# Ending each layer's down projection by token halves, with a norm for each half

## The chip, the cores and the metric

The kernel runs on one core of one Trainium2 chip. The metric is the time of one execution in microseconds of device time, lower is better. The engines are PE (matrix multiply, with its weight loads), DVE (elementwise, reductions), ACT (activations, casts, copies), POOL, and SP, which here only issues DMA transfers. Each engine works through its own instructions in the order in which they were placed, and an instruction that waits holds up those behind it on the same engine.

## The reference

Two layers of a hybrid encoder over 256 tokens of width 2048, float32. Cut to what matters:

```
h = x                                           # (1, 256, 2048)
h = h + pool_mixer(rms_norm(h, norm1_g[0]))     # layer 0
h = h + swiglu_ffn(rms_norm(h, norm2_g[0]))     # w1, w3: 2048 x 5632, w2: 5632 x 2048
h = h + rwkv7_time_mix(rms_norm(h, norm1_g[1])) # layer 1
h = h + swiglu_ffn(rms_norm(h, norm2_g[1]))
return rms_norm(h, final_g)

rms_norm(x, g)   = x * rsqrt(mean(x * x over the width) + 1e-6) * g
swiglu_ffn(h)    = (silu(h @ w1) * (h @ w3)) @ w2
```

The time mixing is six token-shifted mixes, projections by w_r, w_k, w_v, low-rank maps for decay, rate and gate, a recurrence over 256 tokens for 32 heads of size 64 (computed here in chunks, with triangular systems that are inverted step by step), a group norm, a gate and the projection w_o.

## The kernel before

The 256 tokens are two halves i = 0, 1 of 128 rows (partitions), the width four column groups n = 0..3 of 512. `h[i][n]` is a 128x512 tile that stays on the chip from start to end (the trace calls it `base`, like everything in that large buffer). Each float32 operand of a product is split into a high and a low part: a weight tile `raw` (128x1024, loaded on SP's queue at L151, four buffers) is cast to `wh` on ACT (L152) and `wl = raw - wh` is taken on DVE (L153), with two buffers of each (`kwh`, `kwl`, `vh`, `vl` are the same in other buffers). A product is then three matmuls: high by high, low by high, high by low.

`ffn(layer)` ends with the down projection, the loop `for two in range(2)`. One pass makes two column groups n0, n1 for both halves in four accumulators `C[i][m]`, over 22 steps p of 256 rows of w2. Eighteen steps run first (seven of them in a form with fewer products and extra accumulators, which are added to `h` on DVE). The last four, p = 18 to 21, run as `columns(p, m)`: all four for the first column group (m = 0), then all four for the second (m = 1), for both halves at once. Behind each column group stand the additions `h[i][n] += C[i][m]` on DVE (L426) and the sums of squares on ACT (L164, tile `junk`); in the second layer also the multiplication by the final gain (L1101). `rstd_of_h` makes the reciprocal root of both halves in one go: a reduction (L171), a square root on ACT (L172, whose table of functions has to be loaded), a reciprocal and a Newton step on DVE (L173 to L182). `load_sqrt`, right behind the up projections, is there to request that table early; its argument is a constant, so nothing ties it to that place.

After the first layer's FFN, `rwkv` starts with `hs[i] = h[i][n] * rstd`, two PE transposes per block of 128 columns into one PSUM tile, an evacuation with the gain on ACT (L666, 16 of them, 128x256), mixes on DVE and then the projections (PE from L736). Behind the projections, from about 1100 to 1400 us, the recurrence is worked off chunk by chunk beside the projection w_o: `KB` and `AR` are loaded per chunk (L832, L833), Gram products `g` and `G` are made, `sv`, `vt`, `rhs`, `cb` are the chunk's vectors, S the state, y the output, which is normed (L976 to L996; `ysq` is its square on ACT, L980) and transposed on PE (L1002). The triangular systems of one half of the chunks are inverted together on DVE: `sysM` is loaded from `dM`, then pairs of L633 (`sysP`) and L634 (`sysZ`) follow one another, and the result goes out to `dZ` and comes back as `Z`.

After the second layer's FFN, `rstd` scales `h` (DVE L1111 for the first half, ACT L1109 for the second) and eight stores of 256 KB go out, four on ACT's queue, four on SP's.

The order on each engine is not written out. A scheduler with its own time model puts the instructions of the whole program in order when the program is built, so an edit in one place can change the order elsewhere.

Of the kernel before, what the change touches and what calls it, by code (L numbers as in the profile page):

```python
# [37 lines left out]
GC, G7 = 1, 0  # L38
# [54 lines left out]
def hybrid_encoder(ctx: ExitStack, tc: tile.TileContext, I, out):  # L93
# [156 lines left out]
    def ffn(layer, each=None):  # L250
        gcol = par[f"g2_{layer}"]
        with ExitStack() as st:
# [4 lines left out]
            rb = base[:, 4864:]  # L257
# [79 lines left out]
            load_sqrt(epsr[:, 0:1])  # L337
# [112 lines left out]
    def rwkv():  # L450
        with ExitStack() as st:
# [192 lines left out]
            with tc.tile_pool(name="rp1", bufs=1) as p1:  # L644
                rstd = rstd_of_h()
                hn = []
                hn_ = p1.tile([128, 16, 257], F32, name="hn")
                for n in range(4):
                    hs = []
                    for i in range(2):  # L650
                        s_ = mx(F32, "hs")
                        if i and n < HSA:
                            nc.scalar.activation(s_, h[i][n], AF.Copy, scale=rstd[:, i:i + 1])
                        else:
                            nc.vector.tensor_scalar(s_, h[i][n], rstd[:, i:i + 1], None, ALU.mult)
                        hs.append(s_)
                        nc.sync.dma_start(dH[i][n], h[i][n])
                    for q in range(4):
                        k = n * 4 + q
                        tp = g_bank()  # L660
                        for i in range(2):
                            nc.tensor.transpose(tp[:, i * 128:(i + 1) * 128], hs[i][:, q * 128:(q + 1) * 128], ident)
                        t_ = hn_[:, k]
                        with queued("newton"):
# [501 lines left out]
```

## Time and profile before

| | us |
|---|---|
| three runs | 2180.53, 2188.81, 2189.13 (median 2188.81) |
| profiled execution | 2181.9 |
| its span in the trace | 2180.1 |
| mean granted TensorE clock | 0.981 of full |
| PE busy | 2116.9 (97% of the span) |
| DVE busy | 1553.9 (71%) |
| ACT busy | 1147.3 (53%) |
| last matmul of the first down projection | starts at 780.61 |
| stretch of the recurrence | about 1100 to 1400 |
| last matmul of the program | starts at 2166.50 |

A row of the trace's order in time gives the start in us, the duration, engine, line, operation, out<-in, the shape and how many such instructions were joined in the row; in brackets stands the idle time of the engine just before it and what ended that. A clock of 1.00 is TensorE's level of 2.4 GHz, 0.50 that of 1.2 GHz.

### The profile page before, as it was taken

To read this page: it belongs to the slowest core of one execution; us is meant where nothing else is said; L and a number is where in the kernel's file an instruction comes from. 1 tells how busy PE (TensorE), PEld (TensorE's weight loads), DVE (VectorE), ACT (ScalarE), POOL (GpSimd) and SP (SyncE) were. 2 spreads that over 40 slices of the span, in tenths; PEclk is the share of its full clock that TensorE was granted. 3 is DMA by queue.
4 is the path that set the end of the run, shared out by engine and by line. 5 is a ranking of instruction groups with operands and counts; after the bars stand their busy time and mean duration, and the time that the engine had idled before them with its cause. 6 is when DMAs were issued, how large, how long until landed. Compare 5 with 4: busy or idle time off the path is not lost.

```text
span 2180.1 us, 34748 instructions
## 1 busy us (share of the span) xinstructions
PE 2116.9 (97%) x13318; PEld 1843.5 (85%) x13318; DVE 1553.9 (71%) x2548; ACT 1147.3 (53%) x1884; POOL 30.6 (1%) x72
## 2 busy tenths in 40 slices
PE   7999999999999989999999999999999999999997
PEld 5888888888878879999988778788888888888786
DVE  8666666666787978688866767876666666677886
ACT  5544444444555478766745354554444444445444
POOL 0000000000000000011000000000000000000000
PEclk9999999999999999999998699999999999999999
DMA  6555565665566645466565343446666666655654
GB/s 232 174 187 191 186 191 187 190 187 190 196 198 217 207 155 163 163 210 207 171 218 151 108 121 105 160 121 191 188 189 189 188 189 189 188 191 199 204 202 156
DMA packets 147478, 395.11 MB, mean 181 GB/s; under 512 B 39280, under 2 KB 46832, under 8 KB 147056
## 3 DMA queue, kind: packets, MB, share of 16 engines
q1 hardware_dynamic: 146160, 390.80, 56.2%
q8 instruction: 104, 1.70, 0.3%
q10 hardware_dynamic: 1152, 2.10, 0.3%
q14 instruction: 62, 0.51, 0.1%
HBM read 376.59 MB, written 16.25 MB: 180 GB/s over the span
## 4 chain that ended last, share of the span: by engine, by line
PE 86%; DVE 6%; DMA 4%; ACT 2%; issue 1%; SPq 0%; ACTq 0%; DVEq 0%
PE acc L311 29%; PE acc L347 17%; PE acc L313 15%; PE acc L691 2%; PE acc L689 2%; PE acc L690 2%; DVE wl L153 2%; PE tp L347 2%; PE acc L1022 1%; PE acc L1024 1%; PE acc L1023 1%; DMA raw<-in_w 1%; PE acc L516 1%; PE acc L515 1%; PE cb L907 1%
## 5 line engine op out<-in xcount | busy, mean ns | idle before, releaser
L153 DVE TENSOR_TENSOR wl<-raw,wh 128x1024 fp32r<-128x1024 f32 (+1 forms) x525 | 640.2, 1220 | 432.2 <-ACT wh L152 428.0
L152 ACT CAST wh<-raw 128x1024 fp32r<-128x1024 f32 (+1 forms) x525 | 548.5, 1045 | 648.7 <-PE acc L311 276.9
L311 PE MATMUL acc<-xs,wh 128*128 128x512 f32 x2816 | 710.6, 393 | 3.7 <-DVE xs L266 3.2
L311 PEld LDWEIGHTS acc<-xs,wh 128*128 128x128 f32 x2816 | 504.9, 189 | 94.9 <-DVE xs L266 5.1
L313 PEld LDWEIGHTS acc<-xs,wl 128*128 128x128 f32 x2816 | 384.1, 190 | 27.5
L313 PE MATMUL acc<-xs,wl 128*128 128x256 f32 x2816 | 392.7, 282 | 0.0
L347 PE MATMUL acc<-vh,gT 128*128 128x512 f32 x640 | 184.9, 390 | 0.8 <-ACT vh L152 0.8
L347 PEld LDWEIGHTS acc<-vh,gT 128*128 128x128 f32 x640 | 119.7, 188 | 27.3 <-ACT vh L152 2.6
L691 PE MATMUL acc<-mx,wl 128*128 128x256 f32 x464 | 133.0, 287 | 3.5 <-DVE wl L153 3.5
L689 PE MATMUL acc<-mx,wh 128*128 128x256 f32 x464 | 132.1, 285 | 0.0
L690 PE MATMUL acc<-mx,wh 128*128 128x256 f32 x464 | 131.8, 284 | 0.0
L153 DVE TENSOR_TENSOR vl<-raw,vh 128x1024 fp32r<-128x1024 f32 x80 | 95.5, 1221 | 27.1 <-ACT vh L152 19.7
L347 PE MATMUL acc<-vl,gT 128*128 128x512 f32 x320 | 112.2, 389 | 0.0
L152 ACT CAST vh<-raw 128x1024 fp32r<-128x1024 f32 x80 | 80.9, 1050 | 49.3 <-PE acc L347 22.7
L355 ACT CAST vh<-T 128x1024 fp32r<-128x1024 f32 x56 | 58.9, 1052 | 80.5 <-DVE T L397 43.6
L347 PE MATMUL acc<-wh,gT 128*128 128x512 f32 x320 | 93.8, 390 | 0.7 <-ACT wh L152 0.7
L691 PEld LDWEIGHTS acc<-mx,wl 128*128 128x128 f32 x464 | 88.5, 191 | 5.3 <-DVE wl L153 5.2
L689 PEld LDWEIGHTS acc<-mx,wh 128*128 128x128 f32 x464 | 88.5, 191 | 0.8
L690 PEld LDWEIGHTS acc<-mx,wh 128*128 128x128 f32 x464 | 88.6, 191 | 0.0
L347 PE MATMUL acc<-vh,g 128*128 128x512 f32 x280 | 77.9, 391 | 1.1 <-ACT vh L355 0.6
L516 PE MATMUL acc<-wl,mx 128*128 128x256 f32 x256 | 74.2, 290 | 1.2 <-DVE wl L153 1.1
L515 PE MATMUL acc<-wh,mx 128*128 128x256 f32 x256 | 74.2, 290 | 0.0
(329 smaller groups left out, 3118.5 us busy)
## 6 DMA issues: line engine op xcount, KB each, us to landing
raw<-in_w SPq DMA_DIRECT2D x528, 512.0 KB, 4.4
raw<-in_wk SPq DMA_DIRECT2D x32, 512.0 KB, 3.7
raw<-in_wr SPq DMA_DIRECT2D x32, 512.0 KB, 3.7
raw<-in_wv SPq DMA_DIRECT2D x32, 512.0 KB, 4.0
raw<-in_wo SPq DMA_DIRECT2D x32, 512.0 KB, 3.6
raw<-in_pw SPq DMA_DIRECT2D x8, 512.0 KB, 7.8
dKB<-KB SPq DMA_DIRECT2D x16, 256.0 KB, 3.1
dKB<-AR SPq DMA_DIRECT2D x16, 256.0 KB, 3.7
```

The lines of the kernel that those rows point to most:

```text
L152: nc.scalar.copy(wh[:P, :step], raw[:P, :step])
L153: nc.vector.tensor_sub(wl[:P, :step], raw[:P, :step], wh[:P, :step].bitcast(F32))
L311: nc.tensor.matmul(acc, lhsT=w[:, cs], rhs=xs[q * 4 + kk], start=(q + kk == 0), stop=False, skip_group_check=True)
L313: nc.tensor.matmul(acc[:, :256], lhsT=l[:, cs], rhs=xs[q * 4 + kk][:, :256], start=False, stop=(q + kk == 6), skip_group_check=True)
L347: nc.tensor.matmul(out_, lhsT=lhsT, rhs=rhs, start=start, stop=stop, skip_group_check=True)
L355: nc.scalar.copy(wh, src)
L515: nc.tensor.matmul(av[:, i], lhsT=xh, rhs=w[:, cs], start=(k == 0 and i == 0), stop=False, skip_group_check=True)
L516: nc.tensor.matmul(av[:, i], lhsT=xh, rhs=l[:, cs], start=False, stop=False, skip_group_check=True)
L689: nc.tensor.matmul(acc[:, :256], lhsT=w[:, cs], rhs=xs[k][:, :256], start=(k == 0), stop=False)
L690: nc.tensor.matmul(acc[:, :256], lhsT=w[:, cs], rhs=xs[k][:, 256:], start=False, stop=False)
L691: nc.tensor.matmul(acc[:, :256], lhsT=l[:, cs], rhs=xs[k][:, :256], start=False, stop=(k == 15))
L907: nc.tensor.matmul(cb[:, jj, 0, hc], lhsT=g_[jj][u % 2][k_, c], rhs=rows_of(u)[k_], start=(u == 0), stop=False, skip_group_check=True)
```

## The change

In the last pass of each down projection the last LH steps (two in the first FFN, one in the second) change their order: the split weights of these steps are kept, and all their products for the first 128 tokens stand ahead of all those for the second. Each half then gets its own additions, squares and `rstd` (one column instead of two), in both layers. The scaling after the first FFN, the transposes and the evacuation go by halves too: four transposes of one half fill a PSUM tile, six of the eight tiles are evacuated on DVE by one multiplication with a broadcast gain (L685, 128x4x128), the other two on ACT by four activations each (L683). At the end the scalings and stores go by halves, with odd column groups on ACT and SP's queue. The gain is multiplied per half, too. `load_sqrt` now takes a value from the last `gT` tile, which ties the request of the root's table to the end of the up projections.

```diff
-GC, G7 = 1, 0
+GC, G7, LH = 1, 0, (2, 1)
-    def rstd_of_h():
-        at = 4624 + 4 * next(counter)
-        s, r = base[:, at:at + 2], base[:, at + 2:at + 4]
-        nc.vector.tensor_reduce(s, ssp, AX.X, ALU.add)
+    def rstd_of_h(i=None):
+        at, w = 4624 + 4 * next(counter), 2 if i is None else 1
+        s, r = base[:, at:at + w], base[:, at + 2:at + 2 + w]
+        nc.vector.tensor_reduce(s, ssp if i is None else ssp[:, i:i + 1], AX.X, ALU.add)
...
-            load_sqrt(epsr[:, 0:1])
+            load_sqrt(gT[FT - 1][0][0][:, 0:1].bitcast(F32))
...
+            def finish(i, n, acc):
+                nc.vector.tensor_add(h[i][n], h[i][n], acc)
+                square_sums(i, n)
+                if each is not None:
+                    each(i, n, lambda: ff.tile([128, 512], F32, name="g4" if n % 2 else "t4", tag="g4" if n % 2 else "t4", bufs=1))
...
-                for m, n in enumerate((n0, n1)):
-                    for p in range(ENDS, FT // 2):
-                        columns(p, m, p == FT // 2 - 1)
-                    for i in range(2):
-                        nc.vector.tensor_add(h[i][n], h[i][n], C[i][m])
-                        square_sums(i, n)
-                    if each is not None:
-                        each(n, ff.tile([128, 512], F32, name="t4", tag="t4", bufs=1))
+                if two == 0:
+                    for m, n in enumerate((n0, n1)):
+                        for p in range(ENDS, FT // 2):
+                            columns(p, m, p == FT // 2 - 1)
+                        for i in range(2):
+                            finish(i, n, C[i][m])
+                    continue
+                for p in range(ENDS, FT // 2 - LH[layer]):
+                    for m in range(2):
+                        columns(p, m)
+                kept = [(p, m, halves(split_weights(src(p, m), tiles=pair_of_v if p % 2 == 0 else None)[0])) for p in range(FT // 2 - LH[layer], FT // 2) for m in range(2)]
+                rstds = []
+                for i in range(2):
+                    for p, m, ws in kept:
+                        for q, w in enumerate(ws):
+                            run(times(C[i][m], gT[2 * p + q][i], *w, False, p == FT // 2 - 1 and q == 1))
+                    for m, n in enumerate((n0, n1)):
+                        finish(i, n, C[i][m])
+                    rstds.append(rstd_of_h(i))
+                return rstds
...
-                for n in range(4):
-                    hs = []
-                    for i in range(2):
+                for i in range(2):
+                    for n in range(4):
                         s_ = mx(F32, "hs")
-                        if i and n < HSA:
-                            nc.scalar.activation(s_, h[i][n], AF.Copy, scale=rstd[:, i:i + 1])
+                        if n % 2 or not i:
+                            nc.scalar.activation(s_, h[i][n], AF.Copy, scale=rstds[i])
...
+                        to = slice(1 + i * 128, 129 + i * 128)
+                        if n % 2 and i:
+                            for q in range(4):
+                                k = n * 4 + q
+                                nc.scalar.activation(hn_[:, k, to], tp[:, q * 128:(q + 1) * 128], AF.Copy, scale=gain[:, k:k + 1])
+                        else:
+                            nc.vector.tensor_mul(hn_[:, n * 4:n * 4 + 4, to], tp.rearrange("p (q c) -> p q c", q=4),
+                                                 gain[:, n * 4:n * 4 + 4, None].broadcast_to((128, 4, 128)))
...
-        ffn(1, times_gain)
-        rstd = rstd_of_h()
+    rstds = ffn(1, times_gain)
+    for i in range(2):
         for n in range(4):
-            for i in range(2):
-                o = h[i][n]
-                if i:
-                    nc.scalar.activation(o, o, AF.Copy, scale=rstd[:, i:i + 1])
-                else:
-                    nc.vector.tensor_scalar(o, o, rstd[:, i:i + 1], None, ALU.mult)
-                (nc.sync if i else nc.scalar).dma_start(out[i * 128:(i + 1) * 128, n * 512:(n + 1) * 512], o)
+            o = h[i][n]
+            if n % 2:
+                nc.scalar.activation(o, o, AF.Copy, scale=rstds[i])
+            else:
+                nc.vector.tensor_scalar(o, o, rstds[i], None, ALU.mult)
+            (nc.sync if n % 2 else nc.scalar).dma_start(out[i * 128:(i + 1) * 128, n * 512:(n + 1) * 512], o)
```

What the built programs place in which order, at three places. The first is PE at the very end of the second FFN in the changed program, its last twelve rows: acc_20712 is C[0][0], acc_20713 is C[0][1], acc_20714 is C[1][0] and acc_20715 is C[1][1]; `x2` is two matmuls.

```order
L348 MATMUL acc_20712<-wl_21558,gT_19808 128x512
L348 MATMUL acc_20714<-wl_21558,gT_19705 128x512
L348 MATMUL acc_20714<-wh_21557,gT_19808 128x512 x2
L348 MATMUL acc_20714<-wl_21558,gT_19808 128x512
L348 MATMUL acc_20713<-wh_21563,gT_19705 128x512 x2
L348 MATMUL acc_20715<-wh_21563,gT_19705 128x512 x2
L348 MATMUL acc_20713<-wl_21564,gT_19705 128x512
L348 MATMUL acc_20713<-wh_21563,gT_19808 128x512 x2
L348 MATMUL acc_20713<-wl_21564,gT_19808 128x512
L348 MATMUL acc_20715<-wl_21564,gT_19705 128x512
L348 MATMUL acc_20715<-wh_21563,gT_19808 128x512 x2
L348 MATMUL acc_20715<-wl_21564,gT_19808 128x512
```

The scheduler has put the two halves of the last step back beside each other: the first half's last accumulator C[0][1] is complete four matmuls ahead of the program's last one.

DVE behind it, to the scalings, in the changed program (L363 adds an accumulator, L1123 multiplies by the gain, L172 to L183 are the two norms, L1132 the scaling):

```order
L363 TENSOR_TENSOR base<-base,acc 128x512 x2
L1123 TENSOR_TENSOR base<-base,t_21583 128x512
L363 TENSOR_TENSOR base<-base,acc 128x512 x2
L1123 TENSOR_TENSOR base<-base,g_21589 128x512
L172 TENSOR_REDUCE base<-base 128x1
L1123 TENSOR_TENSOR base<-base,t_21583 128x512
L1123 TENSOR_TENSOR base<-base,g_21589 128x512
L172 TENSOR_REDUCE base<-base 128x1
L174 RECIPROCAL base<-base 128x1
```

All four additions and all four gains now stand ahead of the first reciprocal. Before, two of the four additions and gains belonged to the column group m = 0, which was complete four steps earlier.

The second place is ACT at the end of the first FFN, from the last casts of w2 and of the next weights to the first scaling. Before:

```order
L152 CAST kwh<-raw 128x1024
L152 CAST wh<-raw 128x1024 x2
L152 CAST kwh<-raw 128x1024 x2
L152 CAST wh<-raw 128x1024 x2
L164 ACTIVATE junk,base<-base 128x512 x2
L172 ACT_TABLE_LOAD
L172 ACTIVATE base<-base 128x2
L653 ACTIVATE hs<-base 128x512
```

With the change:

```order
L152 CAST kwh<-raw 128x1024 x3
L152 CAST wh<-raw 128x1024
L164 ACTIVATE junk,base<-base 128x512
L152 CAST wh<-raw 128x1024 x2
L164 ACTIVATE junk,base<-base 128x512 x3
L173 ACTIVATE base<-base 128x1 x2
L672 ACTIVATE hs<-base 128x512 x6
L683 ACTIVATE hn<-g,base 128x128 x8
```

The table load has left this place, and two casts for the next projections still stand ahead of the last squares, of which there are now three instead of two.

The third place lies in the recurrence, at the second inversion. SP before, from the load of the systems on:

```order
L624 DMA sysM<-dM_6937 32x32x32 x4
L1066 DMA base<-dH_6945 128x512
L869 DMA m_12804<-dM_6936 32x8x32 x2
L973 DMA base<-in_rows 128x256
L832 DMA KB<-dKB_6926 128x512
L833 DMA AR<-dKB_6926 128x512
L151 DMA raw<-in_wo 128x1024
L867 DMA w_12803<-dW_6940 32x8x32 x2
```

And with the change:

```order
L644 DMA sysM<-dM_6951 32x32x32 x4
L1087 DMA base<-dH_6959 128x512
L890 DMA m_12786<-dM_6950 32x8x32 x2
L853 DMA KB<-dKB_6940 128x512
L854 DMA AR<-dKB_6940 128x512
L888 DMA w_12785<-dW_6954 32x8x32 x2
L151 DMA raw<-in_wo 128x1024
L994 DMA base<-in_rows 128x256
```

The chunk's load of KB and AR has moved ahead of the load of `base` from `in_rows`. ACT at the same place before:

```order
L936 ACTIVATE Se<-S,misc 128x128
L844 ACTIVATE KBT<-g,misc 128x2x128 x2
L937 COPY y<-cb 64x256
L912 COPY rhs<-cb 64x256
L844 ACTIVATE KBT<-g,misc 128x2x128 x2
L980 ACTIVATE ysq<-y 128x512
L917 COPY sv<-cb 64x256
L990 ACT_TABLE_LOAD
```

And with the change:

```order
L957 ACTIVATE Se<-S,misc 128x128
L865 ACTIVATE KBT<-g,misc 128x2x128 x2
L958 COPY y<-cb 64x256
L933 COPY rhs<-cb 64x256
L938 COPY sv<-cb 64x256
L865 ACTIVATE KBT<-g,misc 128x2x128 x2
L1001 ACTIVATE ysq<-y 128x512
L1011 ACT_TABLE_LOAD
```

The copy `sv` has moved from behind `ysq` to ahead of it. On DVE the rows from the first `sysP` to the last `sysZ` of this inversion number 100 before and 131 with the change: 31 rows of other work have come to stand between them. No line of the diff lies in this part of the program.

## Rows read from the trace of the kernel before

**Rows 1.** The page: busy time, share of the span and count of each engine.

```profile
PE 2116.9 (97%) x13318; PEld 1843.5 (85%) x13318; DVE 1553.9 (71%) x2548; ACT 1147.3 (53%) x1884; POOL 30.6 (1%) x72
```

**Rows 2.** Waits of PE in the whole span: line, what it waited for, us, times, longest.

```profile
PE g L662 <- DVE hs L655: 8.1, 1, 8.1
...
PE cb L921 <- ACT sv L917: 4.0, 1, 4.0
```

**Rows 3.** Stretches: length, busy time of PE, PEld, DVE, ACT, POOL, granted clock, DMA.

```profile
1183.50:1217.00 33.50, 27.61 (x203) 23.15 (x202) 25.57 (x72) 10.63 (x25) 0.75 (x1) 0.50 0.27 72
1235.00:1251.50 16.50, 16.12 (x90) 13.34 (x91) 6.83 (x17) 5.16 (x13) 0.00 (x0) 0.50 0.39 108
```

**Rows 4.** PE in order of time, at the second inversion and at the first use of its result.

```profile
1181.54 0.66 PE L840 MATMUL g<-base,KB 128*128 128x128 f32 x4 [0.79 <-DMA KB<-dKB]
...
1190.29 1.11 PE L921 MATMUL cb<-sv,base 64*64 64x64 f32 x8 [4.01 <-ACT sv L917]
...
1201.51 1.11 PE L840 MATMUL g<-base,KB 128*128 128x128 f32 x4 [1.88 <-DMA KB<-dKB]
...
1254.06 0.68 PE L916 MATMUL cb<-rhs,Z 64*64 64x64 f32 x8
```

**Rows 5.** ACT in order of time, in the first of these waits.

```profile
1189.35 0.63 ACT L980 ACTIVATE ysq<-y 128x512 f32<-128x512 f32 x1 [6.22 <-DVE sysZ L634]
1189.88 0.35 ACT L917 COPY sv<-cb 64x256 f32<-64x256 f32 x1
```

**Rows 6.** DVE in order of time, the inversion's first and last instruction.

```profile
1188.29 0.21 DVE L633 TENSOR_TENSOR sysP<-sysM,sysZ 128x31 f32<-128x31 f32 x1 [7.32 <-DMA sysM<-dM]
...
1232.82 0.19 DVE L634 TENSOR_TENSOR sysZ<-sysZ,sysP 128x31 f32<-128x31 f32 x1
```

**Rows 7.** SP's queue in order of time, in the same stretch.

```profile
1197.22 0.35 SPq L973 DMA_DIRECT2D base<-in_rows  x1
1197.61 0.44 SPq L832 DMA_DIRECT2D KB<-dKB  x1
...
1241.67 1.44 SPq L864 DMA_DIRECT2D Z<-dZ  x3
```

**Rows 8.** PE in order of time, from the first down projection to the next projections.

```profile
774.70 1.20 PE L347 MATMUL acc<-wh,gT 128*128 128x512 f32 x4 [0.65 <-ACT wh L152]
...
780.61 0.39 PE L347 MATMUL acc<-wl,gT 128*128 128x512 f32 x1
789.11 4.53 PE L662 MATMUL g<-base,hs 128*128 128x128 f32 x20 [8.11 <-DVE hs L655]
793.29 0.78 PE L736 MATMUL acc<-mx,kwh 128*128 128x256 f32 x2
```

**Rows 9.** ACT in order of time, between these projections.

```profile
782.95 1.04 ACT L152 CAST wh<-raw 128x1024 fp32r<-128x1024 f32 x1 [0.24 <-DMA raw<-in_wk]
...
785.36 0.63 ACT L164 ACTIVATE junk<-base 128x512 f32<-128x512 f32 x1
785.89 0.19 ACT L164 ACTIVATION_READ_ACCUMULATOR junk<-base 128x1 f32 x1
786.10 1.28 ACT L172 ACT_TABLE_LOAD   x1
787.39 0.30 ACT L172 ACTIVATE base<-base 128x2 f32<-128x2 f32 x1
```

**Rows 10.** The end of the program in order of time: PE, DVE and ACT.

```profile
2166.50 0.39 PE L347 MATMUL acc<-wl,gT 128*128 128x512 f32 x1
...
2167.72 1.37 DVE L1101 TENSOR_TENSOR base<-base,t 128x512 f32<-128x512 f32 x2
...
2170.86 1.68 DVE L1111 TENSOR_SCALAR base<-base 128x512 f32<-128x512 f32 x4
...
2168.38 1.28 ACT L172 ACT_TABLE_LOAD   x1
...
2171.38 0.35 ACTq L1112 DMA_DIRECT2D out<-base  x1
```

More of the change, by code (lines that the diff above doesn't have):

```diff
@@ L256, in ffn @@
             ps = st.enter_context(tc.tile_pool(name="fps", bufs=1, space=PSUM))
-            rb = base[:, 4864:]
+            rb = base[:, 4864:5120]
             xs = []
@@ L448, in chained, with rwkv @@
             yield from gen
-    def rwkv():
+    def rwkv(rstds):
         with ExitStack() as st:
@@ L644, in rwkv @@
             with tc.tile_pool(name="rp1", bufs=1) as p1:
-                rstd = rstd_of_h()
-                hn = []
                 hn_ = p1.tile([128, 16, 257], F32, name="hn")
-                for n in range(4):
-                    hs = []
-                    for i in range(2):
+                hn = [hn_[:, k] for k in range(16)]
+                gain = par["g1_1"]
+                for i in range(2):
+                    for n in range(4):
                         s_ = mx(F32, "hs")
-                        if i and n < HSA:
-                            nc.scalar.activation(s_, h[i][n], AF.Copy, scale=rstd[:, i:i + 1])
-                        else:
-                            nc.vector.tensor_scalar(s_, h[i][n], rstd[:, i:i + 1], None, ALU.mult)
-                        hs.append(s_)
+                        if n % 2 or not i:
+                            nc.scalar.activation(s_, h[i][n], AF.Copy, scale=rstds[i])
+                        else:
+                            nc.vector.tensor_scalar(s_, h[i][n], rstds[i], None, ALU.mult)
@@ L657, in rwkv @@
                         nc.sync.dma_start(dH[i][n], h[i][n])
-                    for q in range(4):
-                        k = n * 4 + q
                         tp = g_bank()
-                        for i in range(2):
-                            nc.tensor.transpose(tp[:, i * 128:(i + 1) * 128], hs[i][:, q * 128:(q + 1) * 128], ident)
-                        t_ = hn_[:, k]
-                        with queued("newton"):
-                            nc.vector.memset(t_[:, 0:1], 0.0)
-                        nc.scalar.activation(t_[:, 1:], tp[:, :256], AF.Copy, scale=par["g1_1"][:, k:k + 1])
-                        hn.append(t_)
+                        for q in range(4):
+                            nc.tensor.transpose(tp[:, q * 128:(q + 1) * 128], s_[:, q * 128:(q + 1) * 128], ident)
@@ new lines, in rwkv @@
+                        to = slice(1 + i * 128, 129 + i * 128)
+                        if n % 2 and i:
+                            for q in range(4):
+                                k = n * 4 + q
[3 more added lines that the diff above has]
+                                                 gain[:, n * 4:n * 4 + 4, None].broadcast_to((128, 4, 128)))
@@ L669, in mix_tile @@
+                with queued("newton"):
+                    nc.vector.memset(hn_[:, :, 0:1], 0.0)
                 def mix_tile(name, k):
@@ L1093, in hybrid_encoder, with times_gain @@
     pool_layer()
-    ffn(0)
-    rwkv()
-    if True:
-        def times_gain(n, fgB):
-            with queued("load"):
-                nc.sync.dma_start(fgB, I["rows"][3, n * 512:(n + 1) * 512].partition_broadcast(128))
-            for i in range(2):
-                nc.vector.tensor_mul(h[i][n], h[i][n], fgB)
-        ffn(1, times_gain)
-        rstd = rstd_of_h()
-        for n in range(4):
-            for i in range(2):
-                o = h[i][n]
-                if i:
-                    nc.scalar.activation(o, o, AF.Copy, scale=rstd[:, i:i + 1])
-                else:
-                    nc.vector.tensor_scalar(o, o, rstd[:, i:i + 1], None, ALU.mult)
-                (nc.sync if i else nc.scalar).dma_start(out[i * 128:(i + 1) * 128, n * 512:(n + 1) * 512], o)
+    rwkv(ffn(0))
+    gains = {}
+    def times_gain(i, n, place):
+        if n not in gains:
+            gains[n] = place()
+            with queued("load"):
+                nc.sync.dma_start(gains[n], I["rows"][3, n * 512:(n + 1) * 512].partition_broadcast(128))
+        nc.vector.tensor_mul(h[i][n], h[i][n], gains[n])
+    rstds = ffn(1, times_gain)
+    for i in range(2):
+        for n in range(4):
+            o = h[i][n]
[4 more added lines that the diff above has]
+            (nc.sync if n % 2 else nc.scalar).dma_start(out[i * 128:(i + 1) * 128, n * 512:(n + 1) * 512], o)
 def _layout(inp):
```

## The prediction

> **What bounds the kernel now.** I read the engines' totals first: PE is busy for 97% of the span [rows 1], so only what shortens PE's idle time, the end behind its last matmul or its stretches at the lower clock can shorten the kernel. The second view is the list of PE's waits: the largest that the change touches is the 8.1 us between the first FFN and the next projections, where PE waits for the scaled `hs`; the 4.0 us for `sv` lies in the recurrence [rows 2]. The third is the table of stretches with the granted clock: in the recurrence PE runs 33.5 us and again 16.5 us at 0.50, the level of 1.2 GHz, being busy 27.6 and 16.1 us of them [rows 3]. At full clock that work would take half, so these two stretches hold some 22 us. Then I read each place in order of time.
>
> **The end of the program.** Before, the last matmul ends at 2166.89 and the first scaling starts at 2170.86, 3.97 us later [rows 10]. Two things run beside each other in it: the gains of the last column group (two in 1.37 us on DVE) and the table load on ACT (1.28 us, to 2169.66), and the load ends later. The changed order does not separate the halves: C[0][1] is complete four matmuls ahead of the end, at some 0.23 us each, so the first half wins 0.9 us at most. With the table requested earlier, 1.28 us leave ACT's chain. But the column group m = 0, which was finished four steps earlier, now ends with the other, and its gains come late too: DVE has to do the two last additions and then three gains (0.69 each) ahead of the first reciprocal, about 0.7 + 2.1 + 0.3 us for two reductions behind the last matmul, then the two Newton chains, interleaved. For a chain I take the time from the root's end at 787.69 to the transposes at 789.11, less a scaling of 0.42 (a quarter of 1.68): 1.0 us [rows 8 to 10]. Together 4.1 us against 3.97: **no change**, between -1.3 (the whole load is won, the gains hide) and +1.0 (the second chain is not interleaved). From the first store at 2171.38 to the span's end at 2180.1 are 8.7 us for eight stores; the second half's scaling comes one chain later at most, far less than that, so I keep this part.
>
> **The table load.** In the rows, the accumulator is read until 786.08, the load starts at 786.10, and the root follows at 787.39, at once behind it: the price is 1.28 us [rows 9]. The Trainium skill (ScalarE: Activation LUTs, "What ACT_TABLE_LOAD costs") gives 1283 ns for the load, which the row confirms, and a further 1380 ns for a drain, which no gap in these rows shows; by it each end would win 1.4 us more and the sum below would be about -9. I go by the rows. The load is moved behind the last `gT` cast, where DVE and ACT feed PE for the next steps; I cost it at nothing there, and at 1.28 us twice if PE has no products left to cover it.
>
> **The end of the first FFN.** PE's wait of 0.65 us at 774.70 may go, since the casts of w2 now stand in another order: -0.3, between -0.65 and 0 [rows 8]. Then 8.11 us pass from the last matmul's end (781.0) to the first transpose. ACT's casts of the next weights end at 783.99 [rows 9], and in the changed order two of them still stand ahead of three squares (before: two squares). A square with its reading takes 0.75 us (785.36 to 786.08 and the start of the next), so the squares end about 786.3, two roots of 0.30 follow in place of load and root, then the chains: the transposes start between 788.9 and 790.4, which is -0.2 to +1.3. I take +0.5. PE then did 20 transposes in 4.18 us (789.11 to 793.29, 0.21 each) before the first projection; now all 32 stand ahead, 2.5 us more. The 12 need not be done later, where the clock was back and they took half: -1.25. The new evacuation (DVE, 128x4x128 from PSUM with a broadcast gain) has no row; the nearest is the 128x512 gain with 0.69, so six cost 4.1 us on DVE beside 6.7 us of transposes, and hide. If they took twice that, 1.6 us would show. Sum for this end: -0.3 + 0.5 + 1.25 = **+1.4**, between -0.9 and +3.5.
>
> **The recurrence.** The diff touches no line here, but the order changes at the second inversion, and this is the largest term. What happens before: DVE's first `sysP` waits 7.32 us for `sysM`, to 1188.29 [rows 6]. On ACT `ysq` is released by an instruction of that inversion at 1189.35, after 6.22 us, and the copy `sv`, queued behind it, comes at 1189.88 [rows 5]; so PE waits 4.01 us for `sv` [rows 4]. On SP the load of KB stands behind `base` from `in_rows`, which waits until 1197.22; KB is requested at 1197.61 [rows 7], and PE waits 1.88 us for it at 1201.51 [rows 4]. In the changed order `sv` stands ahead of `ysq` and KB ahead of `base`. What `sv` needs is PE's `cb`, done long before, so both waits should go: **-5.9**. What is late next is the normed y, which is still behind the inversion's DMA on DVE; PE has some 14 us of other work ahead of its transposes, so it should not wait.
>
> The clock comes on top. It was low from 1183.5 to 1217, with both waits inside [rows 3, 4]. If PE works through, it can come back sooner. The bounds are 0 (it stays low as long) and 11 us (it is low only for the 5.5 us that it took after 789.11, half of 27.6 less half of 5.5). The nearest row is the second low stretch, where PE was busy nearly throughout and still ran 16.5 us at 0.50 [rows 3]. With 16.5 instead of 33.5 us, 8.3 us would be lost instead of 13.8: -5.5, and I take **-5**. Against it stand waits that the trace can't show: 31 more DVE rows lie between the inversion's start and end, and the work from 1200 to 1300 us is in another order as well. From 0 to 7 us (the idle time of this first stretch and the time around it, 33.5 - 27.6 = 5.9, and one wait as at 1181.54), I take **+3.5**.
>
> **Sum.** 0 + 1.4 - 5.9 - 5 + 3.5 = -6.0 us. On the profiled execution's 2181.9 that is 2175.9, on the median of the three runs (2188.81) 2182.8. Both levels occur among the runs (2180.53 and 2189.13), so I set the time between: **2179 us**.
>
> **Rivals.** (1) *The clock stays up in the recurrence.* No new waits, and the clock back 5.5 us after the fall: 1.4 - 5.9 - 11 = -15.5, 2166 to 2173 us. For it: both waits lie within the first low stretch. Against: a low stretch of 16.5 us with PE busy. (2) *Nothing is won in the recurrence*, since each wait removed there comes back further on, behind DVE: DVE was busy 25.6 of 33.5 us in that stretch, near its limit if PE goes faster [rows 3]. Then only the ends are left, +1.4: 2182 to 2190. (3) *The inversion comes late, slower.* It took 44.7 us for 100 rows (1188.29 to 1233.0), 0.45 each; 31 more make 14 us [rows 6]. Its result was requested until 1243.1 and used at 1254.06 [rows 4, 7], so 11 us were spare, and PE comes there up to 11 us sooner. The changed order asks for it one chunk later, which should cover this. If that chunk's work is less than the missing 14 us, PE stands up to 14 us, and the clock falls for another 16.5 us at a cost of 8. That would be -5.9 + 1.4 + 14 + 8 = +17 at the worst, and it ends slower than before from about 5 us of such waiting on: 2187 to 2200. (4) *The change does what it says at both ends*: the halves overlap, the load's 1.28 us are won at the end and the first FFN's end loses nothing: -2 beside the forecast, within its range.
>
> **How the numbers follow.** Forecast, with (4) in it, 2170 to 2188: 0.46. Rival 1: 0.22. Rival 2: 0.20. Rival 3: 0.12. The likeliest gives the time. 8 in 10 need most of rival 1 and the nearer half of rival 3: **2166 to 2194**. A measurement of this kernel can tell about 0.5% from no change, 11 us. Faster by more than that: nearly all of rival 1 (0.20) and the lower edge of the forecast (0.07), 0.27. Slower: the worse part of rival 3, 0.07. Within: 0.66.
>
> **What would show it.** At the end: no table load between the last square and the root, the first scaling 3.9 to 4.3 us behind the last matmul. After the first FFN: transposes 8 to 9.5 us behind the last matmul, the first projection some 15 us behind it (12.3 before). In the recurrence: no wait of PE for `sv` at the second inversion and none for KB behind it; the stretch at clock 0.50 shorter than 33.5 us. The prediction is wrong if PE's idle time from 1180 to 1300 us is not smaller, if new stretches at 0.50 appear there or elsewhere, or if PE waits for a `Z`.

## The result

| | before | with the change |
|---|---|---|
| median of the runs shown with the result, us | 2185.37 (6 runs, 2180.53 to 2191.77) | 2200.98 (6 runs, 2196.85 to 2203.29) |
| span of the profiled execution | 2180.1 | 2200.3 |
| granted clock, mean | 0.981 | 0.978 |

The ratio is 1.0067 (95% interval 1.0043 to 1.0090): the change is slower by some 15 us. The forecast was 2179 us with a range up to 2194; the time lies outside it, on the slow side.

The page of the changed kernel, busy time and the clock by slices of 55 us, answers to [rows 1]:

```profile
PE 2134.7 (97%) x13318; PEld 1860.4 (85%) x13318; DVE 1552.9 (71%) x2546; ACT 1147.4 (52%) x1883; POOL 27.3 (1%) x72
...
PEclk9999999999999999999998789999999999999999
```

PE has the same 13318 matmuls and is busy 17.8 us longer, so most of the 20.2 us of span is longer busy time, not waiting. The time is cut by events that both traces have. The Gram product meant here and below is the first that stands behind 1080 us, the ninth group of its line (eight groups stand between 929 and 1004 us already):

```profile
1087.51 0.46 PE L602 MATMUL g<-AR,KB 64*64 64x64 f32 x16
...
1434.75 0.73 PE L311 MATMUL acc<-xs,wh 128*128 128x512 f32 x2 [0.22 <-DVE xs L266]
```

is before, and with the change:

```profile
1090.49 0.46 PE L622 MATMUL g<-AR,KB 64*64 64x64 f32 x16
...
1457.34 0.73 PE L312 MATMUL acc<-xs,wh 128*128 128x512 f32 x2 [1.36 <-DVE xs L267]
```

| us | before | change | difference |
|---|---|---|---|
| end of first FFN's last matmul to first transpose | 8.11 | 6.27 | -1.8 |
| the same to the first projection | 12.29 | 14.14 | +1.9 |
| first projection to this Gram product (L602, L622) | 294.22 | 294.09 | -0.1 |
| Gram product to the second FFN's first matmul | 347.24 | 366.85 | **+19.6** |
| from there to the last matmul | 731.75 | 729.89 | -1.9 |
| start of the last matmul to the end of the span | 13.59 | 13.12 | -0.5 |

The rest, 1.3 us, lies ahead of the first FFN's end, where the first FFN started 1.4 us later in this execution. The whole loss stands in the recurrence, a part of the program that no line of the diff touches.

The 347.24 and 366.85 us divide into three parts: PE's idle time, what the lower clock takes (half of PE's busy time in the stretches at 0.50) and the busy time that is left, called work below. Before they are 15.3, 27.0 and 305.0 us, with the change 18.1, 36.2 and 312.5: +2.8, +9.2 and +7.5, though the matmuls are the same.

There, what I forecast first did happen. The waits of PE from 1180 to 1300 us in the changed kernel (line, what it waited for, us, times, longest):

```profile
PE g L896 <- DMA w<-dW: 3.2, 1, 3.2
PE cb L928 <- ACT y L958: 2.9, 2, 2.1
PE cb L942 <- ACT sv L938: 2.5, 1, 2.5
PE cb L942 <- ACT vt L938: 1.4, 2, 0.9
PE g L861 <- DMA KB<-dKB: 1.2, 2, 1.0
```

The wait of 4.0 us for `sv` at 1190 [rows 4] is gone from that place, that for KB is down from 1.9 to 1.0, and the first stretch at the lower clock is 14 us long instead of 33.5. Stretches of the changed kernel, to set beside [rows 3] (length, busy PE, PEld, DVE, ACT, POOL, clock, DMA):

```profile
1196.00:1210.00 14.00, 14.00 (x79) 12.14 (x77) 9.53 (x25) 3.39 (x10) 0.61 (x1) 0.52 0.25 81
1233.00:1261.00 28.00, 28.00 (x114) 23.07 (x114) 15.46 (x34) 6.17 (x15) 0.61 (x1) 0.52 0.09 29
```

At the second of the eight groups of transposes of y the change is 6 us ahead (144 us behind the Gram product, before 150). At the third it is 23 us behind (209 against 186). Between them lies a second low stretch, 28 us in which PE is busy throughout, and then this, PE in order of time:

```profile
1273.85 0.68 PE L942 MATMUL cb<-vt,G 64*64 64x64 f32 x8 [0.92 <-ACT vt L938]
...
1277.00 1.10 PE L928 MATMUL cb<-sv,G 64*128 64x64 f32 x8 [2.09 <-ACT y L958]
...
1279.45 1.11 PE L937 MATMUL cb<-rhs,Z 64*64 64x64 f32 x8 [0.46 <-ACT rhs L933]
1283.03 1.11 PE L942 MATMUL cb<-sv,G 64*64 64x64 f32 x8 [2.47 <-ACT sv L938]
1287.34 0.28 PE L896 MATMUL g<-w,m 32*32 32x32 f32 x2 [3.19 <-DMA w<-dW]
```

9.1 us of waits in 14: one chunk's chain, step by step, with no other work beside it in the trace, and at its end PE waits for `w`, a result of the second inversion. Most of the 2.5 us for `sv` come from it too: ACT's copy of the inversion's result stands ahead of the copy `sv`, waits for DVE and takes 1.93 us:

```profile
1280.79 1.93 ACT L658 COPY sysM<-sysZ 64x1024 f32<-64x1024 f32 x1 [1.40 <-DVE sysZ L654]
1282.62 0.36 ACT L938 COPY sv<-cb 64x256 f32<-64x256 f32 x1
```

DVE's first and last instruction of that inversion, and one of the waits between them, answer to [rows 6]:

```profile
1191.92 0.21 DVE L653 TENSOR_TENSOR sysP<-sysM,sysZ 128x31 f32<-128x31 f32 x1 [1.32 <-DMA sysM<-dM]
...
1213.08 1.23 DVE L153 TENSOR_TENSOR wl<-raw,wh 128x1024 fp32r<-128x1024 f32 x1 [5.49 <-ACT wh L152]
...
1280.52 0.19 DVE L654 TENSOR_TENSOR sysZ<-sysZ,sysP 128x31 f32<-128x31 f32 x1
```

The inversion takes 88.6 us instead of 44.5, from the start of its first instruction to that of its last. In it DVE is busy for 61.2 us (38.5 before) and idle for 27.6 (6.2 before). PE's idle time from 1180 to 1300 us is 11.7 us, before 9.8.

### The profile page after: what moved, and what is told of

It is laid out like the page before. It is cut to its first block, busy times and chain, and to the rows that moved or that the text cites. A ratio compares the mean times of both kernels' runs of the same rounds, so it can differ in the third digit from the quotient of the medians.

```text
span 2200.3 us, 34714 instructions
## 1 busy us (share of the span) xinstructions
PE 2134.7 (97%) x13318; PEld 1860.4 (85%) x13318; DVE 1552.9 (71%) x2546; ACT 1147.4 (52%) x1883; POOL 27.3 (1%) x72
## 4 chain that ended last, share of the span: by engine, by line
PE 84%; DVE 7%; DMA 4%; ACT 2%; issue 2%; SPq 0%; ACTq 0%; DVEq 0%
PE acc L312 29%; PE acc L348 16%; PE acc L314 15%; DVE wl L153 2%; PE acc L712 2%; PE acc L710 2%; PE acc L711 2%; PE tp L348 1%; PE cb L928 1%; PE acc L1043 1%; PE g L874 1%; PE acc L1044 1%; PE acc L1045 1%; PE acc L536 1%; DMA raw<-in_w 1%
## 5 line engine op out<-in xcount | busy, mean ns | idle before, releaser
L356 ACT CAST vh<-T 128x1024 fp32r<-128x1024 f32 x56 | 58.9, 1052 | 75.7 <-PE acc L348 42.2
L348 PE MATMUL acc<-wh,gT 128*128 128x512 f32 x304 | 89.0, 390 | 0.7 <-ACT wh L152 0.7
L710 PEld LDWEIGHTS acc<-mx,wh 128*128 128x128 f32 x464 | 88.6, 191 | 0.8
L711 PEld LDWEIGHTS acc<-mx,wh 128*128 128x128 f32 x464 | 88.6, 191 | 0.0
```

The costliest lines, as they stand in the source:

```text
L348: nc.tensor.matmul(out_, lhsT=lhsT, rhs=rhs, start=start, stop=stop, skip_group_check=True)
L356: nc.scalar.copy(wh, src)
L710: nc.tensor.matmul(acc[:, :256], lhsT=w[:, cs], rhs=xs[k][:, :256], start=(k == 0), stop=False)
L711: nc.tensor.matmul(acc[:, :256], lhsT=w[:, cs], rhs=xs[k][:, 256:], start=False, stop=False)
```

## Experiments

A separation by parts came first, then the order itself. "Stretch" is the time from the first Gram product to the second FFN's first matmul in the profiled execution, "parts" are its idle time, its loss to the lower clock and its work, as above; "inversion" is the second one on DVE; the last two columns are the times to the first transpose and the first projection from the end of the first FFN's last matmul. Each row's times are from one execution. One source holds e1, e2, e4 and e10, with switches: H0 and H1 are the matmul order by halves of the first FFN and the end by halves of the second, N0 the norms by halves in the recurrence's front, SQ the later table request.

| kernel | ratio to before | stretch | parts | inversion | transposes | projection |
|---|---|---|---|---|---|---|
| before | 1 | 347.2 | 15.3, 27.0, 305.0 | 44.5 | 8.1 | 12.3 |
| the change | 1.0067 (1.0043 to 1.0090) | 366.9 | 18.1, 36.2, 312.5 | 88.6 | 6.3 | 14.1 |
| e1 no norm halves | 0.9991 (0.9975 to 1.0007) | 348.9 | 15.9, 23.6, 309.4 | 44.2 | 6.3 | 10.4 |
| e2 norm halves only | 0.9992 (0.9973 to 1.0012) | 341.4 | 10.2, 20.2, 311.1 | 68.1 | 8.7 | 15.7 |
| e3 inversion a step earlier | 1.0052 (1.0024 to 1.0080) | 357.4 | 14.3, 31.8, 311.3 | 39.3 | 6.3 | 13.7 |
| e4 tail halves only | 1.0011 (0.9994 to 1.0027) | 348.2 | 17.6, 25.4, 305.3 | 44.5 | 8.0 | 12.2 |
| e5 change, before's order | 0.9981 (0.9954 to 1.0008) | 343.7 | 12.2, 26.5, 305.0 | 44.4 | 6.3 | 14.1 |
| e6 before, change's order | 1.0080 (1.0054 to 1.0106) | 372.6 | 18.6, 41.9, 312.2 | 91.3 | 8.0 | 12.2 |
| e7 inversion pulled up | 1.0100 (1.0042 to 1.0159) | 359.1 | 17.4, 28.3, 313.3 | 37.8 | 6.3 | 14.5 |
| e9 its result, too | 1.0038 (1.0014 to 1.0062) | 358.3 | 16.3, 29.2, 312.8 | 42.2 | 6.3 | 14.5 |
| e10 table request only | 1.0003 (0.9981 to 1.0025) | 352.3 | 14.8, 33.1, 304.4 | 43.7 | 7.0 | 11.2 |
| e8 mixed order | 0.9982 (0.9957 to 1.0007) | 339.9 | 10.0, 18.3, 311.6 | 67.0 | 6.3 | 10.4 |
| e11 the same again | 0.9968 (0.9948 to 0.9988) | 341.6 | 8.7, 21.9, 311.0 | 67.0 | 6.3 | 10.4 |
| e12 before, mixed order | 0.9980 (0.9964 to 0.9996) | 349.6 | 9.2, 30.4, 310.0 | 65.4 | 7.7 | 11.9 |

**e1: without the separate norms.** The part behind the first FFN goes back to one norm for both halves and the old transposes (they stand behind the `else`); the rest of the change stays.

```diff
+H0, N0, H1, SQ = 1, 0, 1, 1
...
-                    rstds.append(rstd_of_h(i))
-                return rstds
+                    if layer or N0:
+                        rstds.append(rstd_of_h(i))
+                return rstds if layer or N0 else rstd_of_h()
...
+                if N0:
...
+                else:
+                    rstd = rstds
```

> The change without the separate norms, scalings, transposes and evacuation by halves after the first FFN; the matmul order of both down projections, the end of the program and the root's table stay as changed. The second inversion then has 100 DVE rows from first sysP to last sysZ, as before (131 with the change). Theory A (the loss is the recurrence's new order, which this part of the change sets off): the time falls back to before's or a little under it, ratio 0.996 to 1.001; the inversion takes 42 to 48 us in the trace, no PE wait over 2 us for w or Z around it. Theory B (the loss comes from the matmul order by halves and the ends): ratio stays near 1.006.

The loss is gone, at 0.9991, with 100 DVE rows in the inversion. So the loss needs this part.

**e2: the separate norms alone**, in the kernel before.

```diff
+H0, N0, H1, SQ = 0, 1, 0, 0
...
+                    if layer == 0 and N0:
+                        return [rstd_of_h(i) for i in range(2)]
...
-    ffn(0)
-    rwkv()
...
+    rwkv(ffn(0))
```

(with the change's scaling, transposes and evacuation inside `rwkv`.)

> The kernel before with only the separate norms, scalings, transposes and evacuation by halves after the first FFN. The second inversion has 118 DVE rows. Theory A: slower than before, ratio 1.003 to 1.009, with most of the difference between the first chunk's Gram products and the first matmul of the second FFN, and an inversion of over 60 us. Theory B: ratio 0.999 to 1.002, only the 1.9 us later first projection.

Theory A in that form missed: the inversion does take 68 us, but the time is that of before, and the stretch is 5.8 us *shorter* in its execution. The part costs 3.4 us where it stands (15.7 against 12.3 us to the first projection) and gets them back. The count of rows in the inversion is no measure of the loss: the order that the scheduler finds for e2 is another one than the change's.

**e3: the second inversion a step earlier**, in the changed kernel.

```diff
-LV, LP, PE_, IE = 6, 14, 8, 16
+LV, LP, PE_, IE = 6, 14, 7, 15
```

> The changed kernel with one constant of the recurrence altered: the second inversion is put into the program one step earlier (PE_ 8 to 7, IE 16 to 15). It has 92 DVE rows then instead of 131; everything else of the change stays. Theory A: most of the 20 us come back, ratio to before 0.995 to 1.001, inversion 40 to 50 us, no idle PE of 10 us behind it. Theory B: ratio stays near 1.006, since ends and halves are unchanged.

Half missed: the inversion takes 39 us, no long wait stands behind it, and the kernel is still slower, 1.0052. PE waits 8.4 us for KB in the stretch (5.2 before), but its idle time there is not longer than before (14.3 against 15.3); the lower clock takes 4.8 us more and the work 6.3. This edit too gave the whole recurrence a new order, so it tells nothing of the inversion by itself; the runs that follow hold the order.

**e4: the second FFN's end by halves alone**, in the kernel before (the last two sections of the diff and the order of the last step's products).

> The kernel before with only the second FFN's end by halves: matmul order of the last step, gains, norms, scaling and stores by halves. The recurrence's order is as before. Both theories: within 0.2% of before. The first scaling comes 3.5 to 4.2 us behind the last matmul (3.97 before, 3.47 with the whole change). The table load stands in the tail again, since its request is not moved: beside the gains, so it may cost up to 1 us against the whole change's tail.

The time is as expected, and the first scaling comes 4.28 us behind the last matmul, just above the range. From the last matmul's start to the end are 14.0 us (13.6 before, 13.1 with the whole change): the halves cost 0.4 us while the table load still stands in the tail.

**e5 and e6: the orders exchanged.** The recurrence is traced alike in both kernels, instruction by instruction, so its order on every engine (2375 instructions on PE, 607 on DVE, 405 on ACT, 198 on SP, 17 on POOL) can be written down from one kernel and held in the other, by edges that fix the order of issue and make no engine wait for another. The array `a` holds one list of instruction numbers for each engine.

```diff
+def pin(tc, nc, off):
...
+    ins = {i.name: i for i in nc.cur_bb.bb.instructions}
+    at = 0
+    for _ in range(5):
+        n = a[at]
+        names = [f"I-{x - off}" for x in a[at + 1:at + 1 + n]]
+        at += 1 + n
+        for p, q in zip(names, names[1:]):
...
+            tc.add_manual_dep(ins[q], p, mybir.DependencyInfo(mybir.DependencyClass.NoSync, mybir.DependencyReason.DATA))
```

> The whole change, with the order of the recurrence's instructions on PE, DVE, ACT, SP and POOL held at that of the kernel before by edges that fix the order of issue and add no wait. Theory A (the loss is the recurrence's order alone): ratio 0.997 to 1.001, and from the first Gram product to the second FFN's first matmul 346 to 350 us (347.2 before, 366.9 with the change). Theory C (the separate norms leave something in the recurrence slower than before whatever its order): ratio stays above 1.004.

> The kernel before, untouched but for the recurrence's order, which is held at that of the changed kernel. Theory A: ratio 1.006 to 1.010, the stretch from Gram product to second FFN 363 to 369 us, an inversion of 80 to 90 us and PE idle about 10 us around its end. Theory C: ratio 0.998 to 1.002.

Both ratios came out as theory A has it. The sizes in the two traces lie a little outside the ranges named: the stretch is 343.7 us (346 to 350 expected) in e5 and 372.6 (363 to 369) in e6, and e6's inversion takes 91.3 (80 to 90). The changed kernel with before's order is no slower than before, and the kernel before, with nothing changed but this order, takes on the whole loss and the picture that goes with it. The work goes with the order too: 305.0 us in e5 as before, 312.2 in e6. The inversion's first and last instruction on DVE, and two of PE's waits, in e6:

```profile
1192.46 0.21 DVE L652 TENSOR_TENSOR sysP<-sysM,sysZ 128x31 f32<-128x31 f32 x1 [1.32 <-DMA base<-dH]
...
1283.76 0.19 DVE L653 TENSOR_TENSOR sysZ<-sysZ,sysP 128x31 f32<-128x31 f32 x1
...
1280.23 1.97 PE L926 MATMUL cb<-sv,G 64*128 64x64 f32 x8 [2.10 <-ACT y L956]
...
1290.60 0.28 PE L894 MATMUL g<-w,m 32*32 32x32 f32 x2 [3.21 <-DMA w<-dW]
```

So the loss is the recurrence's order, and, within these intervals, nothing that the change computes. Why the scheduler finds this order when the norms are separate, no run shows.

**e7: the inversion pulled up.** The changed kernel, its own order held, except that the 62 DVE instructions of the second inversion stand closer: 38 others between them instead of 92.

> The changed kernel in its own order, with the 62 DVE instructions of the second inversion alone pulled up: 38 other instructions lie between them instead of 92 (the other 54 follow in their old sequence). Theory D (PE waits for the inversion's result, because DVE's inversion is queued behind work that waits for PE and ACT): the inversion falls from 88.6 to 45 to 60 us, the 10 us of PE's waits at its end go, ratio to before 0.998 to 1.003. Theory E (the loss is spread over the order, the late inversion is a symptom): ratio stays above 1.005, since new waits of PE for what was moved back take its place.

The stretch falls by 7.8 us in the traced execution, but that is the fastest of four runs (2193 to 2214 us), and the ratio stays at 1.01, where theory E put it: theory D is not enough. The trace gives a reason. SP's and ACT's queue and PE in e7, in order of time:

```profile
1245.13 13.08 SPq L170 DMA_DIRECT2D raw<-in_wo  x4
1258.49 0.33 SPq L1013 DMA_DIRECT2D base<-in_rows  x1
1258.87 0.42 SPq L676 DMA_DIRECT2D dZ<-sysZ  x1
...
1266.78 1.94 ACT L677 COPY sysM<-sysZ 64x1024 f32<-64x1024 f32 x1
...
1273.48 0.28 PE L915 MATMUL g<-w,m 32*32 32x32 f32 x2 [3.34 <-DMA w<-dW]
```

The inversion was done at 1228.7, and its result left at 1258.87, behind four loads that wait for free `raw` buffers; ACT's copy of it comes at 1266.78 behind the casts of those weights. With the inversion done early, the result is still late on two more queues.

**e9: its way out pulled up as well.** As e7, with ACT's copy ahead of the four casts, and dZ, dW and the first loads of Z and w ahead of the four loads.

> As e7 (the changed kernel's own order, the second inversion pulled up on DVE), and the result's way out pulled up too: ACT's copy of it stands ahead of the four casts of w_o's weights, and SP's stores dZ, dW and the first loads of Z and w stand ahead of the four loads of w_o. In e7 the inversion ended at 1228.5, but dZ went out at 1258.87 behind these loads, the copy came at 1266.78, and PE waited 3.3 us for w. Theory F (the result is held by three queues in order, DVE, ACT and SP): no wait of PE for w or Z, the stretch from Gram product to second FFN 350 to 357 us (366.9 with the change, 359.1 in e7). Theory E (the work for w_o that stood in front is what PE lacks later): the wait moves but the stretch stays at 357 to 365.

The wait for `w` is gone, as theory F has it, and the ratio goes to 1.0038, below the change's, though the two intervals overlap. The stretch is 358.3 us, where theory E put it: a wait of 2.1 us for `ys` takes a part back. In the traces of e7 and e9 the early inversion is thus worth about 8 of the 20 us, nearly all of it at the lower clock (36.2 us with the change, 28.3 and 29.2 here); the runs do not confirm this size. What is left of the loss in e9's stretch, 11.1 us against before, is 1.0 us of idle time, 2.2 at the lower clock and 7.8 of work: the early inversion leaves the longer work as it was.

**e10: only the later request of the root's table**, in the kernel before.

```diff
+H0, N0, H1, SQ = 0, 0, 0, 1
...
-            load_sqrt(epsr[:, 0:1])
+            load_sqrt(gT[FT - 1][0][0][:, 0:1].bitcast(F32) if SQ else epsr[:, 0:1])
```

> The kernel before with only the later request of the root's table. The recurrence's order is before's on every engine. Expected of the trace: no table load ahead of either root, the first transpose 6.2 to 6.9 us behind the first FFN's last matmul (8.11 before), the first projection 10.4 to 11.1 us behind it (12.29 before), the first store's lead at the end shorter by up to 0.6 us. Of the time: 1.5 to 2.5 us less than before, ratio 0.998 to 1.000, within what can be told from no change.

Nothing that can be told in the time (1.0003, where 0.998 to 1.000 was expected), but it shows in its place: the transposes start 7.0 us behind the last matmul instead of 8.1, the first projection 11.2 instead of 12.3, and the end is 0.3 us shorter. The first two gains are a little under the lower ends that I had named. The stretch, with before's order, was 352.3 us in this execution; before, e1, e4, e5 and e10 (the same order or nearly) lie between 343.7 and 352.3, so a single profile of this stretch is worth some 4 us either way.

**e8, e11, e12: a better order.** e1's kernel with e2's order held in the recurrence (e8, again with more runs as e11), and the kernel before with that order and nothing else (e12).

> The change without separate norms after the first FFN (as e1) with the recurrence's order held at that of e2 (118 DVE rows). If orders carry their time with them, the recurrence takes 340 to 343 us as in e2, against 348.9 in e1, and the ratio is 0.994 to 0.997, under both kernels. If e2's 341.4 was due to where its PE stood when it came there, it stays at 347 to 350 and the ratio near 0.999.

> The kernel of e8 with more rounds, since it came out under both kernels without being clear of before: 0.9982 (0.9957 to 1.0007) there. If its recurrence of 339.9 us (347.2 before) and its first FFN's end (10.43 us to the first projection against 12.29) hold, the ratio is 0.995 to 0.998 and its interval ends below 1.000.

> The kernel before with nothing of the change, and the recurrence's order held at that of e2, as in e8 and e11. If the gain of e11 is that order and not the change, the stretch from Gram product to second FFN takes 339 to 343 us (347.2 before) and the ratio is 0.996 to 0.999; the first projection stays 12.2 us behind the first FFN's last matmul and the end at 13.6 us, so it lies 2 to 3 us above e11 (0.9968). If e11's gain is the change's, the ratio is 0.999 to 1.001.

e8's 0.9982 lies between the two ranges named, with a stretch of 339.9 us. e11 is faster than before: 2175.87 us against 2182.83, 0.9968, interval clear of 1 and of the change's. The order alone (e12) gives 0.9980, also clear of 1, though its one profile has a stretch of 349.6 us, not the 339 to 343 expected. The rest would be the table request and the ends by halves; the two intervals overlap, so this division is argued, not shown. This order has longer work than before's, too (311.0 us in e11), but less idle time (8.7 against 15.3) and less loss to the lower clock (21.9 against 27.0; 30.4 in e12). The first FFN's end in e11, to be set beside [rows 8]:

```profile
791.52 4.49 PE L740 MATMUL g<-base,hs 128*128 128x128 f32 x20 [6.27 <-DVE hs L733]
795.70 0.56 PE L814 MATMUL acc<-mx,kwh 128*128 128x256 f32 x2
```

## Why the prediction was wrong

**The end of the program: right.** Forecast 0 (-1.3 to +1.0), measured -0.5. The last three instructions that the sum spoke of, in the changed kernel, beside [rows 10]:

```profile
2187.23 0.39 PE L348 MATMUL acc<-wl,gT 128*128 128x512 f32 x1
...
2190.31 0.29 ACT L173 ACTIVATE base<-base 128x1 f32<-128x1 f32 x1 [0.71 <-DVE base L172]
...
2191.09 0.72 ACT L1130 ACTIVATE base<-base 128x512 f32<-128x512 f32 x1 [0.48 <-DVE base L183]
```

The first scaling comes 3.47 us behind the last matmul (3.97 before, 3.9 to 4.3 expected). No load stands ahead of the root, and the gains on DVE end last, as the sum said. DVE is through with additions, gains and reductions 2.7 us behind the last matmul (3.1 in the sum), and from there the first scaling comes after 0.8 us (1.0 in the sum).

**The table load: the row was right.** e10 gains 1.1 us at the first end for a load of 1.28 us, and nothing is seen of a further 1.4 us. The Trainium skill (ScalarE: Activation LUTs, "What ACT_TABLE_LOAD costs") counts 2.66 us for a switch; here the trace disagrees with the part beyond the load itself.

**The end of the first FFN: the sum right, its terms not.** Forecast +1.4, measured +1.9 to the first projection; that these are close is luck, since three terms missed and made up for each other. PE and ACT there in the changed kernel, beside [rows 8, 9]:

```profile
788.52 6.19 PE L678 MATMUL g<-base,hs 128*128 128x128 f32 x32 [6.27 <-ACT hs L672]
796.40 0.50 PE L757 MATMUL acc<-mx,kwh 128*128 128x256 f32 x2 [1.68 <-ACT mx L159]
...
784.32 0.63 ACT L164 ACTIVATE junk<-base 128x512 f32<-128x512 f32 x1 [1.00 <-DVE base L363]
```

The transposes came 1.8 us earlier, not 0.5 later: the casts for the next projections, which I left where they were, ended 1.1 us behind the last matmul (3.0 before), so the squares began sooner. Against it the 32 transposes and what follows took 7.9 us to the first projection, not 6.7: PE waited 1.68 us for the first mix, which I had hidden behind the transposes. And the 12 transposes moved ahead were not given back later (-0.1 instead of -1.25). The wait of 0.65 us that was to go is still there, 0.66 us at 778.68. e1 and e2 price the parts: the separate norms cost 3.4 to 3.7 us here, the other parts win 1.9.

**The recurrence: the step that failed.** Forecast -7.4, measured +19.6. At the place that I had read, the first two terms mostly held: the wait for `sv` went, that for KB fell from 1.9 to 1.0 us, and the first stretch at 0.50 was 14 us instead of 33.5. What failed is that I priced a new order of the whole recurrence by this one place. Over the stretch, idle time was to fall by 2.4 us (-5.9 and +3.5) and rose by 2.8; the term for new waits was bounded by the idle time of the old stretch, and waits came back further on, that for `sv` among them with 2.5 us. The lower clock was to take 5 us less and took 9.2 more, in low stretches behind the first, which the term left out. And PE's work, which the sum took as unchanged without a reason, rose by 7.5 us. All three signs of being wrong that the prediction named appeared: the idle time from 1180 to 1300 us is longer, a stretch at 0.51 stands from 1278 to 1295 us where the mean was 0.80 before, and PE waits for `w`, which like Z is a result of the second inversion.

Rival 3 had a part of the mechanism, at a chance of 0.12; that its +17 at the worst is near what came is partly luck, since it has no longer work in it. It was put too low because I priced the 31 additional rows at 0.45 us each, 14 us, and the inversion grew by 44. The 31 rows are 44 instructions, since like ones are joined in a row. DVE is busy 22.7 us longer in the inversion and idle 21.4 us longer, because some of these instructions wait in DVE's queue for PE and ACT (5.5 us for one `wl` alone). The way out did not add to it here: SP sent dZ at 1280.78, right behind the inversion's end at 1280.71. Only with the inversion pulled up do four loads and four casts stand ahead of the result (e7).

Over the whole trace up to the last matmul, 20.7 us more divide into 2.9 us of idle PE, 9.1 us lost to the lower clock, and 8.7 us of work. So "PE waits for a Z" was only the smaller part. The work is the steadiest of the three: in the stretch it is 304.4 to 305.3 us in the four traces with before's order (before, e4, e5, e10), while the loss to the lower clock is 25.4 to 33.1 there, so the +9.2 us are uncertain by some 4.

The longer work is in the small products. The 1671 matmuls of the stretch whose shape begins with 64 or 32 rows (64*128, 64*64, 32*32), each counted from its start to the next one's and weighted with the clock, take 107.1 us before and 115.6 with the change, 107.0 in e5 and 115.2 in e6. The last section shows a part of it in rows.

## What to carry to other kernels

A scheduler that orders the whole program can answer an edit at one end with another order elsewhere, and that order can be worth more than the edit: here 0.8% (e6), against nothing that can be told for the edit with the old order held (e5). Before a change of order is priced, count what now stands between an instruction and its result on every queue that it passes, and price each of those instructions by what it waits for, not by its duration. Do not take the busy time of an engine as given either: divide it into idle time, loss to the clock and work, and compare all three. To find out whether the edit or the order costs the time, hold the old order under the new code and the new order under the old code; two runs settle it.

## What was not expected of the hardware

PE can be busy without a gap and stay at the lower clock. From 1233 to 1261 us the changed kernel's PE was busy 28.0 of 28.0 us at a mean of 0.52, working through small products (64x64, 64x128) in turn with runs of four to eight 128x512 ones; it rose at 1261.3, within a run of eighteen 128x512 ones that had begun at 1257.89. After 789.11 us in the kernel before it had risen within 5.5 us.

What a small product costs depends on the order on PE as well as on the clock. Gram products of the changed kernel, at 1.00, at 0.50 and again at 1.00, from PE in order of time:

```profile
1214.61 1.16 PE L874 MATMUL g<-AR,KB 64*128 64x128 f32 x16
...
1235.36 2.07 PE L874 MATMUL g<-AR,KB 64*128 64x128 f32 x8
...
1360.63 1.16 PE L874 MATMUL g<-AR,KB 64*128 64x128 f32 x8
```

The sixteen start in twos (1214.83 and 1214.83, 1214.94 and 1214.94), the eight start singly (at 1360.84, 1360.95 and 1361.07 in the last row). So eight single ones take 1.16 us at 1.00 and 2.07 at 0.50, a factor of 1.8 for the clock, and sixteen in twos take no longer than eight single ones. Together that is 0.07 us each against 0.26, a factor of 3.6. The six groups of eight that fell into low stretches with the change all ran singly, and took 12.4 us; the 44 products of before that did took 7.8 (12 in 2.08, 16 in 3.09 and 16 in 2.67 us), 0.18 each, since some of them started in twos. How many run in twos goes with the order: of the 512 products `g<-AR,KB`, 316 start less than 0.06 us ahead of PE's next matmul before and in e5, 287 with the change and in e6. What two neighbours need to run side by side, no run here shows.
